# Decoder block on one core: adaLN shift and scale in groups of feature tiles, 32x32 VectorE transposes, another head order

## The chip, the cores and the metric

The kernel runs on one core of one Trainium2 chip. The time is device microseconds from the first to the last instruction of one launch, with what lies around it; the median of three runs before the change is 348.48 us (348.43 to 349.01). The core has five engines that run side by side, each with its own instruction stream: TensorE (PE, matrix products; the loading of its stationary operand is shown apart as PEld), VectorE (DVE), ScalarE (ACT), GpSimd (POOL) and SyncE (SP), which here only issues transfers from the device memory.

## The reference

One decoder block on 256 tokens of 1024 features, float32, one sequence:

```python
mod = silu(c) @ w_ada + b_ada                      # [6 * 1024], one vector for the sequence
sh1, sc1, gt1, sh2, sc2, gt2 = split(mod, 6)
h = rmsnorm(x, g_mix) * (1 + sc1) + sh1
q, k, v, u, c_gate, b_gate = split(h @ w_in)       # w_in [1024, 3072]
attn = causal attention(q, k, v), 8 heads of 64, with ALiBi slopes
conv = b_gate * causal_conv3(c_gate * u)
x = x + gt1 * (concat(rmsnorm(attn), rmsnorm(conv)) @ w_out)
h = rmsnorm(x, g_ffn) * (1 + sc2) + sh2
val, gte = split(causal_conv3(h @ w_up))           # w_up [1024, 5632]
x = x + gt2 * ((silu(gte) * val) @ w_down)         # w_down [2816, 1024]
return rmsnorm(x, g_final)
```

So every part waits for two things: a number for each token (the reciprocal root mean square) and a number for each feature (shift, scale, gate), which comes from a matrix-vector product with `w_ada` (24 MB in all).

## The kernel before

Everything is held as [feature, token]: the 1024 features are 8 K tiles of 128 partitions, the 256 tokens lie along the row. Large float32 products run as three passes in a faster format: each operand is split into `hi` (rounded; ScalarE makes it) and `lo` (the rest; VectorE makes it), and TensorE adds hi.hi, lo.hi and hi.lo (`mm3`, L200).

The block has three stages. **q, k, v**: K outermost, the 8 feature tiles of q and k and two token tiles of v accumulate in six PSUM banks while the K tiles arrive one after the other. **Mixer**: 12 steps of u, c, b tiles with one attention head beside each of the first eight, then 8 steps of w_out. **FFN**: 66 steps over pieces of w_up and w_down. All orders are written out by hand; each engine runs its instructions in the order of the program text. Weights go through one ring of eight [128, 2048] slots, filled by SP in the order of use; a slot's next transfer is issued once the engines have read its old content (`free`, `advance`).

What the change touches:

* **The head.** x is loaded in four transfers, then the packed parameters `par`. ScalarE squares x (`sqx`, L235), VectorE adds the squares, and TensorE sums them over the partitions (`pss`, L212: stationary the squares, 16 columns of ones moving). VectorE and POOL make the root `r` (L217, L219). To have it on every partition, VectorE multiplies the identity with it (`dg`, L223, two instructions), and TensorE multiplies ones with that (`psrx`, L228). `keep_clock` (L154) issues products whose result nobody reads.
* **adaLN for the mixer.** `ada_rows(kt, r)` (L263) makes one feature tile's shift and scale: silu(c), repeated over 32 columns (`crep`), is stationary, 256 columns of w_ada move. Four products run in the four groups of 32 columns of TensorE's array, each with its own two K tiles. The 512 KB halves of a feature tile's columns take one ring slot each. The result `psr` holds four partial sums in rows: ScalarE copies it to `ar` (L268), `ada_cols` transposes it with two TensorE products with the identity (`psc`, L274), VectorE adds the four (`red`, L276) and makes scale and shift per partition (`mod`, L277, L279).
* **Order in the q, k, v stage.** For each K tile TensorE runs 24 products of 256 columns (q, k) and 6 of 512 (v; one of its banks is named `warm`), and between them, for the next K tile, two calls of `ada_rows` and one `ada_cols`.
* **adaLN for the rest.** `mod_part` (L573) and `gate_part`/`gate_rows` (L553, L561) make sections of 1024 features in the same row form; `mod_copy` (L580) copies, `mod_cols` transposes with two TensorE products (L592) and adds the bias (L597, L601). Three of the four sections are turned in the mixer stage and at the FFN's start, one beside the FFN.
* **The two junctions.** Between mixer and FFN, and at the end, the chain runs pss, ms, r, dg, psrb (L228), then x times the root (`xnf` L285, `xT` L869). VectorE makes a piece of `lo` (L736) in between, or scales x by g_final.

In the tables one float32 product of the program is two MATMUL records and two LDWEIGHTS records; a product in the split format is one each. So the 8 products of an `ada_rows` pair are the 16 records of one L263 group.

Of the kernel before, what the change touches and what calls it, by code (L numbers as in the profile page):

```python
# [8 lines left out]
F32 = mybir.dt.float32  # L9
# [5 lines left out]
P = 128  # L15
S = 256
# [10 lines left out]
# columns of the packed per-feature parameters  # L27
# [8 lines left out]
# [128, 1024] pieces of the weights after q, k, v, in the order in which TensorE takes them  # L36
# [12 lines left out]
ADA_AHEAD = [(0, 0), (1, 1), (2, 2), (3, 3)] + [(k - 1, k) for k in range(4, KT)]  # L49
# [7 lines left out]
def decoder_block(ctx: ExitStack, tc, xT_in, pp, ada1, ada2, wqkv, wst, out):  # L57
    """One adaLN decoder block on 256 tokens, held as [feature, token] throughout.

    Large float32 products run as three float32r passes: an operand v is split exactly into  # L60
    hi = round(v) to float32r and lo = v - hi, which float32r holds too.
    """
# [22 lines left out]
    # ---------------------------------------------------------------- loads  # L85
    xT = cp.tile([P, KT, S], F32, name="xT")
    for i in range(4):
        nc.sync.dma_start(xT[:, 2 * i:2 * i + 2, :], xT_in[:, 2 * i:2 * i + 2, :])
    par = cp.tile([P, NP], F32, name="par")
    ffn_par = slice(PC["ffn_w"], NP)  # L90
    nc.sync.dma_start(par[:, 0:PC["ffn_w"]], pp[:, 0:PC["ffn_w"]])
# [5 lines left out]
    # one ring of [128, 2048] slots, filled in the order of use  # L97
    order = []
    for kt in range(KT):
        order += [("a1", k, i) for k in range(KT) for i in range(2) if ADA_AHEAD[k][i] == kt] + [("q", kt)]  # L100
# [8 lines left out]
    def advance():  # L109
        while state["next"] < len(order):  # L110
# [5 lines left out]
            if k[0] == "a1":  # L116
                nc.sync.dma_start(t[:, 0:1024], ada1[k[1], k[2]])
# [16 lines left out]
    # ------------------------------------------------------------ constants  # L134
# [14 lines left out]
    # TensorE's clock falls when it idles: products for nothing keep it up until the first weights are there  # L149
# [6 lines left out]
    keep_clock(15)  # L156

    # ------------------------------------------------- helpers
# [38 lines left out]
    def mm3(o, l, r, start, stop, shared=False, passes=(0, 1, 2)):  # L197
        """o (+)= (l_hi + l_lo).T @ (r_hi + r_lo) without lo.lo, which is below float32's rounding"""
# [16 lines left out]
    def rms_root(ss, n, name, beside=lambda: None):  # L215
# [4 lines left out]
        beside()  # L220
# [5 lines left out]
    def rms_bcast(dg, ps):  # L226
# [5 lines left out]
    pss = pw("pss")  # L232
    sqx = cp.tile([P, KT, S], F32, tag="mix", name="sqx")
    for i in range(4):
        ACT.activation(sqx[:, 2 * i:2 * i + 2, :], xT[:, 2 * i:2 * i + 2, :], AF.Square)  # L235
        if i:
            DVE.tensor_add(sqx[:, 0:2, :], sqx[:, 0:2, :], sqx[:, 2 * i:2 * i + 2, :])
    DVE.tensor_add(sqx[:, 0, :], sqx[:, 0, :], sqx[:, 1, :])
    add_squares(pss, sqx[:, 0, :], True, True)
    # silu(c), repeated over 32 columns as a stationary operand  # L240
# [8 lines left out]
    dgx = rms_root(pss, D, "x")  # L249
# [3 lines left out]
    mod1 = cp.tile([P, 2, KT], F32, name="mod1")      # scale, shift of the mixer's norm  # L253
# [3 lines left out]
    def ada_rows(kt, r):  # L257
        """half r of the K tiles: the column groups' K tiles are 2 j + r"""
        if r == 0:
            AR[kt] = pw(f"psr{kt}")  # L260
# [671 lines left out]
```

## Time and profile before

| | us |
|---|---|
| median of three runs | 348.48 (348.43 to 349.01) |
| span of the profiled execution | 347.5 |
| PE busy | 335.8 (97%) |
| PEld busy | 312.8 (90%) |
| DVE / ACT / POOL busy | 250.6 / 196.4 / 17.9 |

The profiled execution's own time lies 1.0 us above its span if it was a run of the median. Busy time of PE is not its peak, since products overlap; a stage is read from the starts of its products. The three stages begin at 16.08 us (first q product), 61.66 (first u product) and 147.84 (first product of the FFN); the last product of the FFN starts at 335.83.

### The profile page before, as it was taken

Reading aid. Unit: us, or ns where it says so; the run is one execution under the profiler, and the core shown is the slowest. Engines: PE = TensorE matmul, PEld = TensorE weight load, DVE = VectorE, ACT = ScalarE, POOL = GpSimd, SP = SyncE. Lnnn points to the kernel's source line nnn. Section 1 sums busy time; section 2 is a strip of 40 time slices with the busy share of each in tenths; the row PEclk is TensorE's granted clock in tenths of the full one; section 3 lists DMA queues with packets and bytes.
Section 4 is the critical chain, followed back from the end, with each engine's and each line's share of the span. In section 5 each row is a group of like instructions: output and inputs, shape, how many; then the busy total and the mean of one; then the engine's idle time right before and its main releaser. Section 6 shows DMA issues by size and latency. Waiting matters only on the chain.

```text
span 347.5 us, 6841 instructions
## 1 busy us (share of the span) xinstructions
PE 335.8 (97%) x2812; PEld 312.8 (90%) x2812; DVE 250.6 (72%) x443; ACT 196.4 (57%) x347; POOL 17.9 (5%) x31
## 2 busy tenths in 40 slices
PE   6999999999999999899999999999999999999992
PEld 6777778888788999699999999999999999999992
DVE  2647466497875887689878888888577777777754
ACT  5334355977776455558555555555555555555550
POOL 1000000001112100400000000000000000000020
PEclk9699999999999999999999999999999999999997
DMA  6999899878779567447536675757463642000003
GB/s 231 411 412 356 335 383 421 371 271 320 296 281 409 222 267 258 167 183 238 223 146 257 229 288 205 298 192 307 164 243 129 236 133 111 2 0 2 0 2 121
DMA packets 13854, 79.22 MB, mean 228 GB/s; under 512 B 1664, under 2 KB 2048, under 8 KB 6272
## 3 DMA queue, kind: packets, MB, share of 16 engines
q1 hardware_dynamic: 13824, 78.79, 60.0%
q8 instruction: 22, 0.36, 0.4%
q14 instruction: 8, 0.07, 0.1%
HBM read 77.74 MB, written 1.05 MB: 227 GB/s over the span
## 4 chain that ended last, share of the span: by engine, by line
PE 55%; DVE 1%; ACT 0%; DVEq 0%; issue 0%
PE pu L200 18%; PE pg L200 18%; PE pod L200 18%; PE pss L212 1%; DVE xT L869 1%; PE warm L154 0%; PE psrb L228 0%; DVE lo L736 0%; PE psg L561 0%; ACT hhi L287 0%; DVE xT L691 0%; DVE dg_x L223 0%; DVE xnf L285 0%; ACT sqr L693 0%; DVEq L928 0%
## 5 line engine op out<-in xcount | busy, mean ns | idle before, releaser
L166 DVE TENSOR_TENSOR lo<-raw,hi 128x1024 fp32r<-128x1024 f32 x85 | 103.9, 1228 | 3.0 <-ACT hi L161 3.0
L161 ACT CAST hi<-raw 128x1024 fp32r<-128x1024 f32 x86 | 88.7, 1040 | 0.0
L200 PE MATMUL pu<-hhi,hi 128*128 128x256 f32 x208 | 59.0, 284 | 1.0 <-ACT hhi L287 1.0
L200 PE MATMUL pu<-hhi,lo 128*128 128x256 f32 x208 | 58.2, 280 | 0.0
L200 PE MATMUL pu<-hlo,hi 128*128 128x256 f32 x208 | 57.9, 279 | 0.0
L200 PE MATMUL pod<-ahi,lo 128*128 128x256 f32 x176 | 49.5, 282 | 0.0
L200 PE MATMUL pod<-alo,hi 128*128 128x256 f32 x176 | 49.5, 281 | 0.0
L200 PE MATMUL pod<-ahi,hi 128*128 128x256 f32 x176 | 49.4, 281 | 0.0
L200 PE MATMUL pg<-hhi,hi 128*128 128x256 f32 x176 | 49.4, 280 | 0.0
L200 PE MATMUL pg<-hlo,hi 128*128 128x256 f32 x176 | 49.1, 279 | 0.0
L200 PE MATMUL pg<-hhi,lo 128*128 128x256 f32 x176 | 49.1, 279 | 0.0
L200 PEld LDWEIGHTS pu<-hhi,hi 128*128 128x128 f32 x208 | 39.0, 188 | 2.4 <-ACT hhi L287 1.2
L200 PEld LDWEIGHTS pu<-hhi,lo 128*128 128x128 f32 x208 | 39.1, 188 | 0.0
L200 PEld LDWEIGHTS pu<-hlo,hi 128*128 128x128 f32 x208 | 39.0, 188 | 0.0
L762 DVE SCALAR_TENSOR_TENSOR fyv<-pu,par,fyv 128x255 f32<-128x255 f32 (+1 forms) x44 | 21.2, 482 | 20.7 <-ACT fyv L756 19.9
L756 ACT ACTIVATE fyv<-pu,par 128x256 f32<-128x256 f32 x22 | 12.4, 564 | 40.6 <-PE pu L200 40.6
L200 PEld LDWEIGHTS pod<-ahi,lo 128*128 128x128 f32 x176 | 33.2, 188 | 0.0
L200 PEld LDWEIGHTS pod<-alo,hi 128*128 128x128 f32 x176 | 33.1, 188 | 0.0
L200 PEld LDWEIGHTS pod<-ahi,hi 128*128 128x128 f32 x176 | 33.1, 188 | 0.0
L200 PEld LDWEIGHTS pg<-hhi,lo 128*128 128x128 f32 x176 | 33.1, 188 | 0.0
L200 PEld LDWEIGHTS pg<-hhi,hi 128*128 128x128 f32 x176 | 33.0, 188 | 0.0
L200 PEld LDWEIGHTS pg<-hlo,hi 128*128 128x128 f32 x176 | 32.9, 187 | 0.0
(161 smaller groups left out, 664.4 us busy)
## 6 DMA issues: line engine op xcount, KB each, us to landing
raw<-in_wst SPq DMA_DIRECT2D x43, 1024.0 KB, 4.9
raw<-in_ada SPq DMA_DIRECT2D x16, 1024.0 KB, 6.6
raw<-in_ada SPq DMA_DIRECT2D x16, 512.0 KB, 6.1
raw<-in_wqkv SPq DMA_DIRECT2D x6, 768.0 KB, 7.4
xT<-in_x SPq DMA_DIRECT2D x4, 256.0 KB, 4.6
raw<-in_wqkv SPq DMA_DIRECT2D x2, 512.0 KB, 8.1
out<-xT SPq DMA_DIRECT2D x3, 256.0 KB, 2.7
raw<-in_wqkv SPq DMA_DIRECT2D x2, 256.0 KB, 8.2
```

What stands on the lines that cost most here:

```text
L161: ACT.copy(hi[:, 0:n], raw)
L166: DVE.tensor_sub(lo[:, 0:n], raw, hi[:, 0:n].bitcast(F32))
L200: PE.matmul(o, l[p == 2], r[p == 1], start=start and p == 0, stop=stop and p == 2, skip_group_check=shared)
L212: PE.matmul(ss[:, t * REP:(t + 1) * REP], s2[:, t * P:(t + 1) * P], ones[:, 0:REP], start=(first and t == 0), stop=last, skip_group_check= ...
L756: ACT.activation(Y[w, j], PU[w, j][:, 0:S], AF.Identity, bias=col("ffn_b", f), scale=col("ffn_w", 2 * 2 * NJ + f))
L762: DVE.scalar_tensor_tensor(y[:, d:], ps[:, 0:S - d], col("ffn_w", k * 2 * NJ + f), y[:, d:], op0=OP.mult, op1=OP.add)
L869: DVE.tensor_mul(xT[:, d, :], xT[:, d, :], rb3)
```

## The change

The columns of w_ada are laid out anew on the host, so that a row form of 32 partitions turns into a column form with one VectorE instruction that transposes 32x32 blocks; the TensorE transposes, the ScalarE copies and the reduction go. The mixer's shift and scale are made for groups of feature tiles, (0), (1), (2, 3), (4, 5), (6, 7): every column group of the array now runs over all 8 K tiles and holds 32 of each tile's 128 features, with 64 or 128 columns per product instead of 256. One ring slot holds 1 MB instead of 512 KB of this part. The root is broadcast by a stationary operand that repeats its one column 128 times, with the identity moving. In the head `par` is loaded first and from ScalarE's queue, silu(c) goes ahead of the squares, `ada_rows(0)` ahead of `pss`, and the numbers of clock-keeping products go from 15 and 7 to 22 and 4.

```diff
+GROUPS = [(0,), (1,), (2, 3), (4, 5), (6, 7)]
...
-    nc.sync.dma_start(par[:, 0:PC["ffn_w"]], pp[:, 0:PC["ffn_w"]])
+    nc.scalar.dma_start(par[:, 0:PC["ffn_w"]], pp[:, 0:PC["ffn_w"]])     # ahead of x
...
-        order += [("a1", k, i) for k in range(KT) for i in range(2) if ADA_AHEAD[k][i] == kt] + [("q", kt)]
+    for g, kts in enumerate(GROUPS):
+        order += [("a1", g, i) for i in range(len(kts))] + [("q", kt) for kt in kts]
...
-                nc.sync.dma_start(t[:, 0:1024], ada1[k[1], k[2]])
+                nc.sync.dma_start(t, ada1[GROUPS[k[1]][k[2]]])
...
-    keep_clock(15)
+    keep_clock(22)
...
-        dg = wk.tile([P, 2, P], F32, tag="dg", name=f"dg_{name}")
-        for t in range(2):
-            DVE.tensor_scalar(dg[:, t, :], ident, r[:, t:t + 1], None, op0=OP.mult)
-        return dg
+        return r
...
-            PE.matmul(ps[:, t * P:(t + 1) * P], ones, dg[:, t, :], start=True, stop=True)
+            PE.matmul(ps[:, t * P:(t + 1) * P], r[:, t:t + 1].to_broadcast([P, P]), ident, start=True, stop=True)
...
+    def ada_rows(g):
+        n = len(GROUPS[g])
+        AR[g] = pw(f"psr{g}")[:, 0:64 * n]
+        for k in range(KT):
+            a = ring["a1", g, k * n // KT].rearrange("p (k j c) -> p k j c", j=4, c=64 * n)
+            for j in range(4):
+                PE.matmul(AR[g][32 * j:32 * j + 32, :], crep[:, k, :], a[:, k % (KT // n), j, :],
+                          start=(k == 0), stop=(k == KT - 1))
+            if (k + 1) % (KT // n) == 0:
+                free(("a1", g, k * n // KT))
+    def ada_cols(g):
+        n, kts = len(GROUPS[g]), slice(GROUPS[g][0], GROUPS[g][-1] + 1)
+        tr = wk.tile([P, 256], F32, tag="tr", name=f"tr{g}")[:, 0:64 * n]
+        DVE.transpose(tr, AR[g])
+        v = tr.rearrange("p (n s q) -> p n s q", s=2, q=32)[:, :, :, 0]
+        b = PC["b_ada"] + kts.start
+        DVE.tensor_tensor(mod1[:, 0, kts], v[:, :, 1], bsc1[:, 0, kts], op=OP.add)
+        DVE.tensor_mul(mod1[:, 0, kts], mod1[:, 0, kts], par[:, PC["g_mix"] + kts.start:PC["g_mix"] + kts.stop])
+        DVE.tensor_tensor(mod1[:, 1, kts], v[:, :, 0], par[:, b:b + n], op=OP.add)
...
+    ada_rows(0)
+    add_squares(pss, sqx[:, 0, :], True, True)
+    rx = rms_root(pss, D, "x")
+    ada_cols(0)
+    keep_clock(4)
+    new_q(0)
+    for part in range(3):
+        split_hi_q(0, part)
+    split_lo_q(0, 0)
+    psrx = rms_bcast(rx, pw("psrx"))
     normed(0, psrx)
-    ada_cols(0)
-    keep_clock(7)
-    split_q(0, 0)
     modulated(0)
...
-            qk(kt, range(ROWS_AT[kt], COLS_AT[kt]))
-            if nxt:
-                ada_cols(kt + 1)
+            g = {1: 2, 3: 3, 5: 4}.get(kt)
...
+            if g:
+                ada_rows(g)
+                ada_cols(g)
+            qk(kt, range(4 if kt == 1 else 2, 8))
...
     def mod_cols(s):
-        for i in range(2):
-            PE.transpose(ps[:, i * P:(i + 1) * P], sacc[s, "ar"][:, i * P:(i + 1) * P], ident)
+        tr = wk.tile([P, 256], F32, tag="tr", name=f"trm{s}")
+        DVE.transpose(tr, sacc[s][:, 0:256])
+        v = tr.rearrange("p (k q) -> p k q", q=32)[:, :, 0]
...
-    dg2 = rms_root(pss2, D, "x2", lambda: lo_half(0))
+    r2 = rms_root(pss2, D, "x2")
+    lo_half(0)
+    mod_cols(1)
     lo_half(1)
...
-    h_scaled(0, rb2, mod2, "f", lambda: mod_cols(1))
+    h_scaled(0, rb2, mod2, "f")
```

On TensorE, the head up to the first q and k products stands before as follows (`warm` is the target of the clock-keeping products, `psr` the rows of shift and scale, `psc` their transposes, `pq` the banks of q and k):

```order
L154 MATMUL warm<-ones 128x128 x15
L212 MATMUL pss<-ones,sqx 128x16 x2
L263 MATMUL psr_168<-raw,crep 32x256 x8
L228 MATMUL psrx<-dg_x,ones 128x128 x2
L274 MATMUL psc_188<-ident,ar_181 128x128 x2
L154 MATMUL warm<-ones 128x128 x7
L200 MATMUL pq_163<-hhi,hi 128x256 x2
```

After the change the same place on TensorE reads:

```order
L155 MATMUL warm<-ones 128x128 x22
L261 MATMUL psr_165<-raw,crep 32x64 x32
L213 MATMUL pss<-ones,sqx 128x16 x2
L155 MATMUL warm<-ones 128x128 x4
L226 MATMUL psrx<-ident,r_x 128x128 x2
L201 MATMUL pq_161<-hhi,hi 128x256 x2
```

The rows of shift and scale moved ahead of the sum of squares and are 32 products of 64 columns instead of 8 of 256; the transposes are gone, and the broadcast is the last thing before q and k.

In the q, k, v stage, TensorE's work at the start of the third K tile reads before (`psr_367` are the rows of the fourth feature tile, `pq` again the banks of q and k):

```order
L200 MATMUL pq_163<-hhi,hi 128x256
L200 MATMUL pq_163<-hlo,hi 128x256
L200 MATMUL pq_163<-hhi,lo 128x256
L263 MATMUL psr_367<-raw,crep 32x256 x8
L200 MATMUL pq_164<-hhi,hi 128x256
L200 MATMUL pq_164<-hlo,hi 128x256
L200 MATMUL pq_164<-hhi,lo 128x256
```

After the change rows of two feature tiles stand in the second, fourth and sixth K tile only; in the second they read:

```order
L201 MATMUL pq_161<-hhi,lo 128x256 x2
L201 MATMUL pq_162<-hhi,lo 128x256 x2
L261 MATMUL psr_340<-raw,crep 32x128 x32
L201 MATMUL pq_163<-hhi,hi 128x256
L201 MATMUL pq_163<-hlo,hi 128x256
L201 MATMUL pq_163<-hhi,lo 128x256
```

Two groups of 8 products of 256 columns became one of 32 products of 128 columns, and no transposes follow on TensorE.

## Rows read from the trace of the kernel before

**Rows 1.** The page: its first line and the granted TensorE clock in 40 slices.
```profile
span 347.5 us, 6841 instructions
PEclk9699999999999999999999999999999999999997
```

**Rows 2.** Stretch, length, busy us (records) of PE, PEld, DVE, ACT, POOL; clock, DMA, GB/s.
```profile
16.05:61.80 45.75, 45.75 (x371) 35.88 (x370) 27.33 (x68) 21.30 (x42) 0.00 (x0) 1.00 0.97 383
5.70:9.10 3.40, 1.43 (x14) 1.24 (x12) 2.50 (x4) 3.10 (x5) 0.00 (x0) 1.00 0.98 363
9.10:12.50 3.40, 3.40 (x22) 2.09 (x23) 1.09 (x6) 0.65 (x3) 0.71 (x1) 0.50 1.04 419
...
145.60:149.05 3.45, 2.14 (x17) 1.90 (x17) 3.21 (x9) 1.47 (x4) 0.00 (x0) 1.00 0.86 313
```

**Rows 3.** Timeline of PE in the q, k, v stage: start us, length, what, records.
```profile
23.68 1.07 PE L263 MATMUL psr<-raw,crep 128*32 128x256 f32 x16
...
39.66 0.64 PE L263 MATMUL psr<-raw,crep 128*32 128x256 f32 x8
...
42.72 0.28 PE L200 MATMUL pq<-hhi,lo 128*128 128x256 f32 x1
42.84 0.38 PE L274 MATMUL psc<-ident,ar 128*128 128x128 f32 x2
42.97 0.36 PE L200 MATMUL pq<-hhi,hi 128*128 128x256 f32 x1
43.17 0.28 PE L200 MATMUL pq<-hlo,hi 128*128 128x256 f32 x1
...
45.62 0.64 PE L263 MATMUL psr<-raw,crep 128*32 128x256 f32 x8
...
57.43 0.28 PE L200 MATMUL pq<-hhi,hi 128*128 128x256 f32 x1
...
61.66 0.28 PE L200 MATMUL pu<-hhi,hi 128*128 128x256 f32 x1
```

**Rows 4.** Tile psr: weight loads, duration ns min/median/max, first and last start.
```profile
L263 PEld LDWEIGHTS psr<-raw,crep x128: 106/109/178, 10.0 to 53.1; 128*32 128x32 f32 x128
```

**Rows 5.** Timeline of the head, all engines; idle before and its releaser in brackets.
```profile
1.51 5.60 PE L154 MATMUL warm<-ones 128*128 128x128 f32 x30 [1.51 <-POOL mhalf L140]
10.05 1.94 PE L263 MATMUL psr<-raw,crep 128*32 128x256 f32 x16
10.47 0.71 POOL L219 TENSOR_TENSOR r_x<-ms_x,mhalf 128x2 f32<-128x2 f32 x1 [8.45 <-DVE ms_x L217]
13.18 0.42 DVE L295 TENSOR_TENSOR xna<-xT,psrx 128x256 f32<-128x256 f32 x1 [1.48 <-PE psrx L228]
13.36 2.97 PE L154 MATMUL warm<-ones 128*128 128x128 f32 x14
14.18 0.60 ACT L299 ACTIVATE hhi<-xna,mod 128x256 fp32r<-128x256 f32 x1 [1.24 <-DVE mod L279]
16.08 1.16 PE L200 MATMUL pq<-hhi,hi 128*128 128x256 f32 x8
```

**Rows 6.** Transfers issued at 3.5 us: tile 0's second w_ada half, us to landing.
```profile
raw<-in_ada SPq DMA_DIRECT2D x1, 512.0 KB, 6.5
```

**Rows 7.** Timeline of the junction at the end of the kernel.
```profile
338.68 1.58 PE L154 MATMUL warm<-ones 128*128 128x128 f32 x12
339.10 0.74 POOL L219 TENSOR_TENSOR r_x<-ms_x,mhalf 128x2 f32<-128x2 f32 x1 [2.15 <-DVE ms_x L217]
339.88 0.48 DVE L223 TENSOR_SCALAR dg_x<-ident,r_x 128x128 f32<-128x128 f32 x2
341.05 2.74 DVE L869 TENSOR_TENSOR xT<-xT,psrb 128x256 f32<-128x256 f32 x8 [0.68 <-PE psrb L228]
```

**Rows 8.** Timeline of the junction between mixer and FFN.
```profile
146.00 0.69 DVE L736 TENSOR_TENSOR lo<-raw,hi 128x512 fp32r<-128x512 f32 x1
147.28 0.91 ACT L287 ACTIVATE hhi<-xnf,mod 128x256 fp32r<-128x256 f32 x2 [1.24 <-DVE mod L601]
```

More of the change, by code (lines that the diff above doesn't have):

```diff
@@ L86, in decoder_block @@
     xT = cp.tile([P, KT, S], F32, name="xT")
+    par = cp.tile([P, NP], F32, name="par")
+    ffn_par = slice(PC["ffn_w"], NP)
+    nc.scalar.dma_start(par[:, 0:PC["ffn_w"]], pp[:, 0:PC["ffn_w"]])
     for i in range(4):
         nc.sync.dma_start(xT[:, 2 * i:2 * i + 2, :], xT_in[:, 2 * i:2 * i + 2, :])
-    par = cp.tile([P, NP], F32, name="par")
-    ffn_par = slice(PC["ffn_w"], NP)
-    nc.sync.dma_start(par[:, 0:PC["ffn_w"]], pp[:, 0:PC["ffn_w"]])
     def col(name, i):
@@ L219, in rms_root, with rms_bcast @@
         POOL.tensor_tensor(r, ms, mhalf, op=OP.pow)
-        beside()
-        dg = wk.tile([P, 2, P], F32, tag="dg", name=f"dg_{name}")
+        return r
+    def rms_bcast(r, ps):
         for t in range(2):
-            DVE.tensor_scalar(dg[:, t, :], ident, r[:, t:t + 1], None, op0=OP.mult)
-        return dg
-    def rms_bcast(dg, ps):
-        for t in range(2):
-            PE.matmul(ps[:, t * P:(t + 1) * P], ones, dg[:, t, :], start=True, stop=True)
-        return ps[:, 0:S]
[L232 to L239, printed above, removed]
+            PE.matmul(ps[:, t * P:(t + 1) * P], r[:, t:t + 1].to_broadcast([P, P]), ident, start=True, stop=True)
+        return ps[:, 0:S]
     cs = cp.tile([P, KT], F32, name="cs")
@@ L247, in decoder_block @@
     DVE.tensor_scalar(bsc1[:, 1, :], par[:, PC["b_ada"] + 32:PC["b_ada"] + 40], 1.0, None, op0=OP.add)
-    dgx = rms_root(pss, D, "x")
+    pss = p1("v", "pss")
+    sqx = cp.tile([P, KT, S], F32, tag="mix", name="sqx")
+    for i in range(4):
+        ACT.activation(sqx[:, 2 * i:2 * i + 2, :], xT[:, 2 * i:2 * i + 2, :], AF.Square)
+        if i:
+            DVE.tensor_add(sqx[:, 0:2, :], sqx[:, 0:2, :], sqx[:, 2 * i:2 * i + 2, :])
+    DVE.tensor_add(sqx[:, 0, :], sqx[:, 0, :], sqx[:, 1, :])
     rxb = cp.tile([P, S], F32, tag="sqs0", name="rxb")
@@ L255, in decoder_block @@
     AR = {}
-    def ada_rows(kt, r):
-        if r == 0:
-            AR[kt] = pw(f"psr{kt}")
-        a = ring["a1", kt, r].rearrange("p (k n) -> p k n", n=256)
-        for j in range(4):
-            PE.matmul(AR[kt][32 * j:32 * j + 32, 0:256], crep[:, 2 * j + r, :], a[:, j, :],
-                      start=(r == 0), stop=(r == 1))
-        free(("a1", kt, r))
-        if r == 1:
-            ar = wk.tile([P, 256], F32, tag="ar", name=f"ar{kt}")
-            ACT.copy(ar, AR[kt][:, 0:256])
-            AR[kt] = ar
-    def ada_cols(kt):
-        ps = pw(f"psc{kt}")
-        for i in range(2):
-            PE.transpose(ps[:, i * P:(i + 1) * P], AR[kt][:, i * P:(i + 1) * P], ident)
-        red = wk.tile([P, 2], F32, tag="red", name=f"red{kt}")
-        DVE.tensor_reduce(red, ps[:, 0:256].rearrange("p (i j r) -> p i j r", i=2, j=4)[:, :, :, 0], AX, OP.add)
-        DVE.scalar_tensor_tensor(mod1[:, 0, kt:kt + 1], red[:, 1:2], bsc1[:, 0, kt:kt + 1], col("g_mix", kt),
-                                 op0=OP.add, op1=OP.mult)
-        DVE.tensor_scalar(mod1[:, 1, kt:kt + 1], red[:, 0:1], col("b_ada", kt), None, op0=OP.add)
+    def ada_rows(g):
[17 more added lines that the diff above has]
+        DVE.tensor_tensor(mod1[:, 1, kts], v[:, :, 0], par[:, b:b + n], op=OP.add)
     XN = {}
@@ L305, in decoder_block, with new_q @@
     pq = [acc(f"pq{i}") for i in range(4)]
-    pv = [p1("v", "pv0"), warm]
+    pv = []
     WQ = {}
+    def new_q(kt):
+        WQ[kt] = [hip.tile([P, 1024], F32R, tag=t, name=t) for t in ("hi", "lo", "hi", "lo")]
     def split_q(kt, part):
-        raw = ring["q", kt]
         if part == 0:
-            WQ[kt] = [hip.tile([P, 1024], F32R, tag=t, name=t) for t in ("hi", "lo", "hi", "lo")]
-        hi, lo = WQ[kt][part // 2 * 2:part // 2 * 2 + 2]
-        c = slice((part % 2) * 512, (part % 2) * 512 + 512)
-        ACT.copy(hi[:, c], raw[:, part * 512:(part + 1) * 512])
-        DVE.tensor_sub(lo[:, c], raw[:, part * 512:(part + 1) * 512], hi[:, c].bitcast(F32))
-        if part == 2:
-            free(("q", kt))
+            new_q(kt)
+        split_hi_q(kt, part)
+        split_lo_q(kt, part)
     def qk(kt, tiles, passes=(0, 1, 2)):
@@ L889, in _arrange @@
     sec = w_ada.reshape(D, 6, D)
[L891 to L896 removed]
+    by_k = sec[:, 0:2].reshape(KT, P, 2, KT, 4, 32).transpose(1, 0, 4, 3, 2, 5)
+    ada1 = []
+    for kts in GROUPS:
+        n = len(kts)
+        a = by_k[:, :, :, kts[0]:kts[-1] + 1]
+        ada1 += [a[:, i * KT // n:(i + 1) * KT // n].reshape(P, 2048) for i in range(n)]
+    ada1 = np.stack(ada1)
+    ada2 = np.stack([sec[:, s].reshape(4, 2, P, KT, 4, 32).transpose(0, 2, 1, 4, 3, 5) for s in (2, 3, 4, 5)])
+    ada2 = ada2.reshape(4, 4, P, 2048)
     wqkv = w_in[:, :3 * A].reshape(KT, P, 3 * A)
```

96 lines of the change are left out of this document (38 added, 58 removed).

## The prediction

> **What bounds the kernel now.** I read the page first: its first line and the clock row say 347.5 us of span, nearly all of it at the full clock except the second slice and the end [rows 1]. Then the table by stretches: from 16 to 62 us, the q, k, v stage, PE is busy without a break and DMA at a share of 0.97, so both are near their limit [rows 2]. Last the timeline of PE there, read by starts, since products overlap: the last K tile, the only one without adaLN work beside it, runs from 57.43 to 61.66, 4.23 us; one with it lasts 5.96 us (39.66 to 45.62) [rows 3]. So the stage is bound by TensorE, and 1.73 us of such a K tile is adaLN. Whatever TensorE does less there moves the end, as the mixer and the FFN behind it are dense on TensorE too.
>
> **The price of adaLN in the loop, before.** Around the transposes three q starts in a row, 42.72, 42.97, 43.17, lie 0.45 us apart in all where two products alone need 0.24 (24 of them and 6 of twice the length make the 4.23): the two transposes cost 0.21. The rest of 1.73, 1.52 us, is two groups of rows, 0.76 each. A merged group of 16 records takes 1.07 us, one of 8 takes 0.64: 8 records more are 0.43, two rounds of four column groups at 0.215 each. So 0.43 of the 0.76 is columns and 0.33 goes into and out of the 32-column form. From 16.08 [rows 5] to 61.66 are 45.58 us; eight K tiles alone are 8 x 4.23 = 33.84; adaLN costs 11.74.
>
> **The price after.** Four groups stay in the loop: one of 64 columns and three of 128, each with 32 products, 64 records, 16 rounds. A round of 128 columns is half of 0.215: 16 x 0.1075 = 1.72. A round of 64 is 0.054, in all 0.86. That is the low end, where only columns count. The next end up: each round waits for its weight loads, which last 0.11 us [rows 4]: 16 x 0.11 = 1.76 for either size. I take 1.75 for 128 columns, where both ends meet, and for 64 the middle, 1.3, since no row is nearer to one end. The far end: each record costs what one costs now, 0.43 / 8 = 0.054 us, whatever its columns: 64 x 0.054 = 3.46. Loop after: 4 x 0.33 + 1.3 + 3 x 1.75 = 7.87, so 11.74 - 7.87 = 3.9 us less.
>
> The Trainium skill ("TensorE: Matmul & The Clock Gate", "Back-to-back issue gap") gives products of up to 64 columns a floor of about 25 ns from start to start. By it a round of four would need 0.1 us and the small group 1.6 us; by columns alone it is 0.86. Rows 3 show 0.054 us per record with 256 columns and can't decide between the two.
>
> **The head.** Before, `hhi`, the first thing the q products need, is ready at 14.78 (14.18 + 0.60), but the 14 records of clock-keeping stand from 13.36 to 16.33 in front of them, at half clock; q starts at 16.08 [rows 5]. After: 44 records instead of 30 keep PE until about 8.7 (1.51 + 5.60 + 14 x 0.12, the 0.12 from the 12 records in rows 7). The columns of tile 0 land, now as one transfer, when their second half does today, 3.5 + 6.5 = 10.0 [rows 6]; `par` ahead of x moves the same bytes. Rows from 10.1 for 1.3 plus 0.1 of change of form: 11.5. `pss`, four records of 0.12: 12.0. ms and hops 0.3, POOL's root 0.71: 13.0. Here `dg` is gone and four records of broadcast follow, 0.48 and 0.25 of tail: 13.75. xna 0.42, hhi 0.60, hops: 14.9. The four keep-clock products end before the root does. VectorE's transposition and three small operations fall beside POOL's root, and the `lo` piece behind them ends at about 13.7; a transposition is not in the trace, its nearest rows are xna (0.42, 256 columns from PSUM) and a tiny operation at 0.16, and from either end the start moves by less than 0.3. Gain 16.08 - 14.9 = 1.2 us, with bounds from 0.8 to 1.6 by the small group's two near ends.
>
> **Later transposes.** The three pairs that stand between dense products (two in the mixer, one beside the FFN) go: 3 x 0.21 = 0.65. VectorE's transposes there take up to 0.42 each beside TensorE; ScalarE loses its copies.
>
> **The end.** `dg` lies on the chain, 0.48, between the root's end (339.84) and the broadcast [rows 7]. After, the broadcast stands behind the clock products, whose 12 records last to about 340.1; with 0.48 and the tail, x is scaled from 340.87 instead of 341.05: 0.2 us, between 0 and 0.48.
>
> **Mixer to FFN.** `dg` leaves VectorE's chain, but the transposition with its addition (0.42 + 0.16) now stands ahead of the second `lo` piece (0.69) and of xnf; hhi came at 147.28 and will come there again, give or take 0.3 [rows 8]. I put 0.
>
> **Sum.** 1.2 + 3.9 + 0.65 + 0.2 = 5.95 off a span of 347.5: 341.55. The median, 348.48, is 0.98 above the span, so 342.5 us. For its own range I take the ends for the small group and the head, 341.3 to 343.8.
>
> **Rivals.**
> *Rounds wait for loads.* Each round lasts 0.11 us [rows 4]. The two small groups, one in the head and one in the loop, cost 1.76 instead of 1.3: 343.4. For it speaks that a load lasts longer than 64 columns need; against it that loads and products overlap in the present groups. By the Trainium skill's floor (same page and section) such a group would take 1.6, nearly this case.
>
> *The clock falls in the head.* Before, from 5.70 to 9.10, PE was busy for 1.43 of 3.40 us, with 2 us of nothing at its end, and was granted 0.50 (1.2 GHz) from 9.10 on, though it was then busy throughout [rows 2]; it was back at 2.4 GHz at 16.05, after the keep-clock products. After, PE has nothing to do from 8.7 to 10.1 and from 13.5 to 14.9. Against it: from 145.60 to 149.05 it was busy 2.14 of 3.45 and kept 1.00. If the clock falls, the broadcast takes 0.5 longer, and the first q products run at half speed for 3 to 4 us, somewhat longer than the keep-clock products needed (2.97 [rows 5]), of which half is lost: 2 us in all, 344.5.
>
> *DMA is late.* The rows of tiles 2 and 3 need both their slots, 6.87 MB in the queue's order (x 1.05, `par` 0.05, four slots of w_ada at 1.05, two of q, k, v weights at 0.79): the first 2.15 MB by 10.0, the other 4.72 MB at 419 GB/s [rows 2] by 21.3. TensorE asks at 14.9 + 4.23 + 0.33 + 1.3 + 1.41 (half a q, k part) = 22.2. A margin of 0.9 us; if transfers ran at the stage's mean of 383 GB/s it would be 0.1 short. All later groups have more. Price: up to 2 us, 344.5.
>
> *Slower: each record costs 0.054 us, however few its columns.* Then five groups of 64 records take 3.46 each. The head starts q 2.16 later than I said, at 17.1, and the loop's adaLN is 4 x (0.33 + 3.46) = 15.2, 3.4 more than now. With 0.85 off behind, 347.5 + 1.0 + 3.4 - 0.85 = 351.05, 352.0 us. It decides from 2.75 us per group, 0.043 per record, on. For it: no row shows PE issuing records faster than this for long, and the records of this part rise from 128 to 320. Against: the 0.215 of a present round is what 256 columns, passed twice, need at 2.4 GHz (512 / 2.4 = 213 ns), so the rate is that of columns.
>
> **How the numbers follow.** Forecast 0.50, loads 0.12, clock 0.20, DMA 0.05, slower 0.13. A measurement tells 0.2%, 0.7 us, from no change. Faster: all but the slower case and a part of the DMA case where other waits add up, 0.85; same 0.02; slower 0.13. The range leaves out the slower case and some 0.07 at both ends: 341.2 to 346.0.
>
> **What would show it.** In the profile after: psr groups of 64 records of 1.3 us (64 columns) and 1.75 us (128), by the starts of the products around them, with K tiles 3, 5, 7 and 8 at 4.23; the first q product at 14.9 and the first u product at 56.5; the clock at 1.00 from 9 to 16 us; the last FFN product 5.75 earlier. I am wrong if a group of 128 columns takes over 2.7 us, if q starts after 16, or if PE waits for a landing before the tiles 2 and 3.

## The result and the profile after

The changed kernel takes 343.42 us (median of 342.16, 343.33, 343.52, 343.58) beside 348.75 for the kernel before (348.43 to 349.46): a ratio of 0.9834 [0.981, 0.9858]. Forecast were 342.5 us, between 341.2 and 346.0. The profiled execution is the one of 342.16 us. The page of the kernel after answers to [rows 1]: the span and the rows of 40 slices for PE and its granted clock.

```profile
span 340.3 us, 7158 instructions
...
PE   8799999999999999899999999999999999999992
...
PEclk9999999999999999999999999999999999999998
```

The second slice, at a mean of 0.6 before, is now at the full clock, as is all the rest up to the last broadcast. By the starts of products, the stages compare so (us):

| | before | after | less | forecast |
|---|---|---|---|---|
| first q product | 16.08 | 14.82 | 1.26 | 1.2 |
| q, k, v, to the first u product | 45.57 | 41.23 | 4.34 | 3.9 |
| mixer, to the first FFN product | 86.19 | 85.54 | 0.65 | 0.42 |
| FFN, to its last product | 187.98 | 187.32 | 0.66 | 0.21 |
| tail | 11.67 | 11.43 | 0.24 | 0.2 |
| span | 347.5 | 340.35 | 7.15 | 5.95 |

First the head, in the timeline of all engines (start and duration in us, engine, line, operation, tiles, count). It answers to [rows 5].

```profile
10.20 1.10 PE L261 MATMUL psr<-raw,crep 128*32 128x64 f32 x64 [1.06 <-DMA raw<-in_ada]
11.23 0.62 PE L213 MATMUL pss<-ones,sqx 128*128 128x16 f32 x4
11.96 0.24 DVE L270 STREAM_TRANSPOSE tr<-psr 128x64 f32<-128x64 f32 x1
12.20 0.70 POOL L220 TENSOR_TENSOR r_x<-ms_x,mhalf 128x2 f32<-128x2 f32 x1 [10.18 <-DVE tr L270]
12.96 0.71 PE L226 MATMUL psrx<-ident,r_x 128*128 128x128 f32 x4
13.71 0.42 DVE L291 TENSOR_TENSOR xna<-xT,psrx 128x256 f32<-128x256 f32 x1 [0.44 <-PE psrx L226]
14.16 0.60 ACT L295 ACTIVATE hhi<-xna,mod 128x256 fp32r<-128x256 f32 x1 [1.14 <-DVE xna L291]
14.82 0.39 PE L201 MATMUL pq<-hhi,hi 128*128 128x256 f32 x1 [1.15 <-ACT hhi L295]
```

The reader is to see the chain landing, rows, `pss`, root, broadcast, `xna`, `hhi`, and that the last bracket of the q product names `hhi`: no clock-keeping product stands before it any more, so POOL's 0.70 and the two hops around `xna` set the time.

Then the loop, in PE's timeline of the same kernel: one group of 64 columns, one of 128, and the first u product. It answers to [rows 3].

```profile
15.96 1.10 PE L261 MATMUL psr<-raw,crep 128*32 128x64 f32 x64
16.99 1.18 PE L201 MATMUL pq<-hlo,hi 128*128 128x256 f32 x8
...
20.30 0.63 PE L201 MATMUL pq<-hhi,hi 128*128 128x256 f32 x4
...
21.80 1.95 PE L261 MATMUL psr<-raw,crep 128*32 128x128 f32 x64
23.69 0.39 PE L201 MATMUL pq<-hhi,hi 128*128 128x256 f32 x1
...
56.05 0.28 PE L201 MATMUL pu<-hhi,hi 128*128 128x256 f32 x1
```

From the first row of a group to the next q product are 1.03 us with 64 columns and 1.89 with 128. The first K tile, which carries the small group, lasts from 14.82 to 20.30, 5.48 us, 1.25 above the 4.23 of one without adaLN.

Between mixer and FFN the timeline after answers to [rows 8]:

```profile
138.20 1.14 POOL L220 TENSOR_TENSOR r_x<-ms_x,mhalf 128x2 f32<-128x2 f32 x1 [1.98 <-DVE ms_x L218]
139.35 0.45 DVE L585 STREAM_TRANSPOSE trm<-psm 128x256 f32<-128x256 f32 x1 [0.56 <-PE psm L574]
139.40 0.71 PE L226 MATMUL psrb<-ident,r_x 128*128 128x128 f32 x4
139.92 0.68 DVE L724 TENSOR_TENSOR lo<-raw,hi 128x512 fp32r<-128x512 f32 x1
140.52 0.87 DVE L281 SCALAR_TENSOR_TENSOR xnf<-xT,mod,psrb 128x256 f32<-128x256 f32 x2
```

The broadcast starts with the root's end and runs beside VectorE's transposition; `xnf` starts as VectorE finishes `lo` (139.92 + 0.68), 0.4 us after TensorE has made `psrb`. At the end, the answer to [rows 7]:

```profile
332.26 0.74 POOL L220 TENSOR_TENSOR r_x<-ms_x,mhalf 128x2 f32<-128x2 f32 x1 [2.20 <-DVE ms_x L218]
333.19 0.61 PE L226 MATMUL psrb<-ident,r_x 128*128 128x128 f32 x4
333.90 0.75 DVE L859 TENSOR_TENSOR xT<-xT,psrb 128x256 f32<-128x256 f32 x2 [0.93 <-PE psrb L226]
```

From the root's end (333.00) to the broadcast is 0.19 us, in place of `dg` and its hop.

So the profiled execution answers to the forecast, but the other three have spans of 341.5 to 341.8, 1.2 to 1.5 us longer, and only means of 0.97 to 0.99 of the granted clock. Where these runs lose, and what the changes of each part are worth by themselves, the experiments have to say. Medians below are over all runs of a kernel, while the ratios leave out runs over 1.5% longer than the kernel's fastest.

### The profile page after: what moved, and what is told of

It reads as the page before. It is cut to its first block, busy times and chain, and to the rows that moved or that the text cites. A ratio compares the mean times of both kernels' runs of the same rounds, so it can differ in the third digit from the quotient of the medians.

```text
span 340.3 us, 7158 instructions
## 1 busy us (share of the span) xinstructions
PE 328.0 (96%) x2988; PEld 312.6 (92%) x2988; DVE 249.7 (73%) x433; ACT 190.9 (56%) x334; POOL 18.9 (6%) x31
## 4 chain that ended last, share of the span: by engine, by line
PE 93%; DMA 2%; DVE 2%; SPq 0%; ACT 0%; issue 0%; POOL 0%; DVEq 0%
PE pu L201 22%; PE pg L201 18%; PE pod L201 18%; PE pq L201 7%; PE pox L201 7%; PE pc L201 4%; PE pb L201 3%; PE psm L574 2%; PE psr L261 2%; DMA raw<-in_ada 2%; PE warm L201 2%; PE pv L201 2%; PE pss L213 1%; PE pss L455 1%; PE pss L454 1%; PE pso L502 1%
## 5 line engine op out<-in xcount | busy, mean ns | idle before, releaser
L752 DVE SCALAR_TENSOR_TENSOR fyv<-pu,par,fyv 128x255 f32<-128x255 f32 (+1 forms) x44 | 21.2, 482 | 22.1 <-ACT fyv L746 21.3
```

The lines of the kernel that those rows point to most:

```text
L752: DVE.scalar_tensor_tensor(y[:, d:], ps[:, 0:S - d], col("ffn_w", k * 2 * NJ + f), y[:, d:], op0=OP.mult, op1=OP.add)
```

## The experiments

**The clock in the head (a_clock).** The changed kernel with more clock-keeping products in the head.

```diff
-    keep_clock(22)
+    keep_clock(26)
...
     psrx = rms_bcast(rx, pw("psrx"))
+    keep_clock(5)
```

> The changed kernel with more clock-keeping products in its two idle stretches of the head: 26 instead of 22 at the start, 5 more between the root's broadcast and the first q product. If the 1.2 us between the profiled execution of the changed kernel (342.2 us) and its other three (343.3 to 343.6) are TensorE's clock falling in the head in most executions, all executions come to 342.0 to 342.4 and the mean granted clock to 0.996. Rival: the difference comes from elsewhere (transfers); then the median stays at 343.4 and the executions go on differing.

Measured: 345.63, 343.57, 346.38, 339.03, 345.59, 343.31 us (median 344.58, ratio 0.9787 [0.9738, 0.9836]). The expectation failed: the runs scatter more than those of the changed kernel. The profiled one starts q at 14.55 and ends the loop at 55.94, both fine; it loses at the two junctions. The table by stretches (busy time of each engine, then the granted clock, DMA share and GB/s), first of this kernel, then of the changed one around the FFN's start:

```profile
139.50:141.65 2.15, 0.67 (x5) 0.48 (x5) 1.93 (x6) 0.73 (x2) 0.00 (x0) 1.00 0.80 316
141.65:145.07 3.42, 3.42 (x17) 3.42 (x18) 3.28 (x8) 1.70 (x4) 0.00 (x0) 0.50 0.96 405
329.50:332.80 3.30, 2.98 (x27) 2.78 (x25) 1.66 (x4) 2.70 (x8) 1.47 (x2) 1.00 0.00 0
332.80:336.00 3.20, 3.20 (x16) 3.20 (x16) 0.94 (x4) 1.24 (x4) 0.74 (x1) 0.50 0.00 0
```
```profile
139.50:141.65 2.15, 0.67 (x5) 0.48 (x5) 1.93 (x6) 0.62 (x2) 0.00 (x0) 1.00 0.76 278
141.65:145.07 3.42, 3.42 (x29) 3.42 (x30) 3.28 (x8) 1.82 (x4) 0.00 (x0) 1.00 1.00 414
```

The code of the junction is the same and PE was busy for the same 0.67 of 2.15 us before it; one run is then granted 0.50 (1.2 GHz) and has 17 products in 3.42 us, the other 1.00 and 29. The FFN takes 188.85 instead of 187.32, the tail 13.51 instead of 11.43: 1.5 and 2.1 us for the two falls.

**One part undone in before, and one part added to it (b_noclock, b_cols).** The kernel before without the seven clock-keeping products ahead of q; and the kernel before with VectorE's transposes for the three later sections.

```diff
-    keep_clock(7)
```
```diff
-    mod_copy(1)
+    mod_cols(1)
...
+        DVE.transpose(tr, sacc[s][:, 0:256])
```

> The kernel before without the 7 clock-keeping products that stand between the mixer's first transposes and the first q products. Both theories: the first q product starts at 14.8 instead of 16.08 us. If the 1.3 us that these products hold up q was all there was to gain in the head, 1.3 us faster than before (347.4). Rival, the clock: without them q runs at half the clock for some 3 to 4 us, and the time is 0.3 to 1.0 us above before (349.0 to 349.7).

> The kernel before, with the three sections behind the q, k, v stage and the FFN's shift turned by 32x32 transposes on VectorE (the layout of these columns changed with it), nothing else of the change. Theory: three pairs of TensorE transposes go from between dense products, 3 x 0.21 = 0.65 us: 347.8 to 348.0. Rival one: the VectorE transposes delay what stands behind them and take it back: no change. Rival two: the whole gain seen behind the q, k, v stage (1.6 us) comes from this part: 347.1.

Measured: 350.20 (348.5 to 350.91), ratio 1.0011 [0.9995, 1.0026], for the first; 349.81 (348.26 to 352.62), 1.0024 [0.9997, 1.0052], for the second. Neither is faster than the kernel before, whose runs beside them have a median of 349.36, so both expectations of a gain (347.4 and 347.8 to 348.0) failed. In the profile of b_noclock q does start right behind `hhi`, but at 16.04: the last squares came 1.6 us later in this execution, and TensorE was at 0.50 from 11.14 to 14.55, so this profile can't show what the products alone cost. b_cols needs 55.68 us from the first u product to the first w_out product, 0.45 less than before with its two transposes (0.42 forecast), and 6.80 from the last w_out product to the first of the FFN, 0.39 more than before, since there `dg` (0.48) and the transposition (0.44) stand in one row on VectorE, ahead of `lo` and `xnf`:

```profile
144.66 0.48 DVE L223 TENSOR_SCALAR dg_x<-ident,r_x 128x128 f32<-128x128 f32 x2 [0.59 <-POOL r_x L219]
145.06 0.44 DVE L584 STREAM_TRANSPOSE trm<-psm 128x256 f32<-128x256 f32 x1
146.22 0.86 DVE L285 SCALAR_TENSOR_TENSOR xnf<-xT,mod,psrb 128x256 f32<-128x256 f32 x2
```

Then its clock falls from 147.74 to 151.15, at the FFN's start.

**What sets the length of a group (a_single).** The changed kernel with eight groups of one feature tile each.

```diff
-GROUPS = [(0,), (1,), (2, 3), (4, 5), (6, 7)]
+GROUPS = [(i,) for i in range(KT)]
```

> The changed kernel with groups of one feature tile throughout: 7 groups of 64 columns in the loop instead of one of 64 and three of 128; same columns, 3 more changes of form, 192 more records. Theory (columns set the rounds, 0.33 us per group for going into and out of the 32-column form): 3 x 0.33 = 1.0 us slower than the changed kernel. Rival, only columns count: no difference. Rival, each record costs time of its own (0.02 us beyond its columns): 3.8 us more, 4.8 us slower in all.

Measured: 343.77 (342.78 to 348.38), ratio 0.9829 [0.9804, 0.9854]; the loop takes 42.17 us, 0.94 more than 41.23. In PE's timeline the groups that carry a single tile last as long as the first:

```profile
21.66 1.10 PE L261 MATMUL psr<-raw,crep 128*32 128x64 f32 x64
22.69 0.39 PE L201 MATMUL pq<-hhi,hi 128*128 128x256 f32 x1
```

Three groups and 192 records more cost 0.94 us, 0.31 a group: that is the change of form alone (0.33 in the prediction). If each record had cost 0.054 us, it would have been 10 us. So columns set the length, and the change of form comes on top.

**The broadcast through dg again (a_dg).**

```diff
-            PE.matmul(ps[:, t * P:(t + 1) * P], r[:, t:t + 1].to_broadcast([P, P]), ident, start=True, stop=True)
+            DVE.tensor_scalar(dg[:, t, :], ident, r[:, t:t + 1], None, op0=OP.mult)
...
+            PE.matmul(ps[:, t * P:(t + 1) * P], ones, dg[:, t, :], start=True, stop=True)
```

> The changed kernel with the root broadcast as before (VectorE scales the identity, dg, 2 x 0.24 us, and ones are stationary). If dg lies on the chain as I reckoned: in the head the broadcast starts 0.5 us later, so the first q product at 15.3 instead of 14.82; at mixer to FFN dg (0.5) is ahead of the broadcast, but the chain there ends in VectorE's second lo piece and xnf, so the first FFN product is 0.3 to 0.5 later against the first u product; at the end 0.2 to 0.3 later. In all 1.0 to 1.3 us longer where the clock is the same. The rival, that dg hides beside POOL and TensorE: the stages last as in the changed kernel, to 0.1.

Measured: 340.1, 343.1, 344.54, 348.33 us, ratio 0.9802 [0.9758, 0.9846]. The profiled run, of 340.1 us, is faster than any of the first four of the changed kernel, though each of the three places is later: q at 15.21 (0.39 later, less than the 0.5 expected), the mixer stage 85.87 (0.33 longer), the tail 11.65 (0.22 longer). The head in its timeline:

```profile
12.28 0.70 POOL L220 TENSOR_TENSOR r_x<-ms_x,mhalf 128x2 f32<-128x2 f32 x1 [10.26 <-DVE tr L276]
13.02 0.48 DVE L226 TENSOR_SCALAR dg_x<-ident,r_x 128x128 f32<-128x128 f32 x2 [0.27 <-POOL r_x L220]
13.36 0.71 PE L232 MATMUL psrx<-dg_x,ones 128*128 128x128 f32 x4 [0.45 <-DVE dg_x L226]
...
15.21 0.39 PE L201 MATMUL pq<-hhi,hi 128*128 128x256 f32 x1 [1.15 <-ACT hhi L301]
```

The root ends 0.08 us later here than in the changed kernel's first profile, so 0.31 of the 0.39 are `dg`. A start of q moves with the landing of the first columns anyway: the unaltered kernel starts it at 14.50 in a_same (below), where they landed at 9.74 instead of 10.06. So leaving `dg` out is worth 0.86 us over the three places; the expected 1.0 to 1.3 were too much. The run is short for another reason: its FFN takes 184.23 us instead of 187.32. Up to `psg3`, the four products of the last gate at 238 us, it keeps step with the changed kernel; behind it a step of 24 products takes 2.72 us instead of 2.83, to the end, at a granted clock of 1.00 in both. Products of 256 columns follow each other at 113.3 ns here and at 117.8 there.

**Is that rhythm the kernel's, or drawn in each run (a_same, a_break)?** The changed kernel once more, unaltered; and the kernel a_keep (below) with four more products in the form of `psg3` early in the FFN.

```diff
+        if n == 6:
+            ps6 = pw("break6")
+            for j in range(4):
+                PE.matmul(ps6[32 * j:32 * j + 32, 0:256], ones[:, 0:32], zt[:, 0, 0:S], start=True, stop=True)
```

> The changed kernel once more, for the spread of its runs. In the profiles so far the products of 256 columns of the FFN follow each other at 117.8 ns up to psg3 (the four products of the last gate), and behind it at 117.8 in some kernels and at 113.3 in others, with the granted clock at 1.00 in both: 187.3 or 184.2 us for the stage. If that rhythm is drawn anew in every run, some of these runs lie 3 us below the others, at 339 to 340. If it belongs to the kernel (the changed one has the slow rhythm, those with other heads the fast one), all lie between 342 and 344.

> The kernel with the products at the junctions, and in the FFN behind the first piece of w_down four more products in the form of psg3 (32 columns stationary, 256 moving), whose result nobody reads. If an interruption of this form lets the rhythm change: products at 113.3 ns from there (158 us) to psg3, 3.1 us less, minus 0.5 for the four products, 338.5 to 339.5 in those runs that keep it behind psg3 too. If the rhythm is set by the place or the time in the run: 117.8 up to psg3 as before, and 0.5 us more than without, 342.2.

Measured: a_same 339.28, 340.13, 340.51, 345.94, 347.5, 347.75 (ratio 0.9732 [0.969, 0.9773]); a_break 342.19 to 343.32 (median 342.65). The tables by stretches, of PE and PEld up to POOL as above, ahead of `psg3` and behind it; first the changed kernel's first profile, then a_same, then a_break:

```profile
165.00:236.00 71.00, 71.00 (x605) 71.00 (x604) 59.87 (x84) 40.00 (x60) 0.00 (x0) 1.00 0.66 242
241.00:320.00 79.00, 79.00 (x673) 79.00 (x673) 56.72 (x84) 44.46 (x65) 0.00 (x0) 1.00 0.28 99
```
```profile
165.00:236.00 71.00, 71.00 (x605) 71.00 (x604) 59.65 (x83) 40.04 (x60) 0.00 (x0) 1.00 0.66 240
241.00:320.00 79.00, 79.00 (x700) 79.00 (x699) 58.92 (x87) 46.49 (x68) 0.00 (x0) 1.00 0.28 101
```
```profile
165.00:236.00 71.00, 71.00 (x629) 71.00 (x628) 60.54 (x86) 40.82 (x60) 0.00 (x0) 1.00 0.66 243
241.00:320.00 79.00, 79.00 (x673) 79.00 (x673) 57.05 (x84) 44.48 (x65) 0.00 (x0) 1.00 0.27 99
```

PE counts as busy throughout and the clock is 1.00 in all six; only the number of products differs: 605 or 629 in 71 us, 673 or 700 in 79. The same program has either rhythm, so behind `psg3` it belongs to the run; in these profiles it changes where a group in column form interrupts the dense products (at 164 us in a_break, at 238 in a_same) and then holds to the next interruption. The slow one costs 3.1 us between `psg3` and the end. In a_break's profile the fast one came at the new group and was lost again at `psg3`; its FFN takes 185.50. None of its six runs comes to the 338.5 to 339.5 expected of one that keeps it, so that the new group is the cause rests on one profile, and what decides the draw isn't settled. The rest of a_same's scatter fits the clock: its profile shows 0.50 from 329.44 to 332.86, and a tail of 12.67, and its three long runs, which have no profile, have mean clocks of 0.975 to 0.985.

**The sum of squares ahead of the rows (a_pss).**

```diff
-    ada_rows(0)
     add_squares(pss, sqx[:, 0, :], True, True)
     rx = rms_root(pss, D, "x")
+    ada_rows(0)
...
-    split_lo_q(0, 0)
     psrx = rms_bcast(rx, pw("psrx"))
     normed(0, psrx)
+    split_lo_q(0, 0)
```

So the edit also puts `xna` ahead of the first `lo` piece; no run parts the two moves.

> The changed kernel with the sum of squares and the root ahead of the rows of tile 0, which land only at 10.06: pss fits in TensorE's wait, and the root (0.7 on POOL) beside the rows. If the head is the chain rows, pss, root, broadcast: first q product at 13.7 to 14.0 instead of 14.82. What the later stage makes of it by the landings: the second half of the columns for tiles 2 and 3 lands at 22.0 and is then asked for at 21.0, so about 1.0 of the gain is given back as a wait in the loop, and the first u product comes within 0.3 of 56.05. By the rival, a loop bound by TensorE alone, the first u product comes at 55.0.

Measured: 341.99 to 345.95, ratio 0.9857 [0.9814, 0.99]. q starts at 13.72, 1.10 earlier (its rows start 0.26 earlier, at 9.94); the first u product comes at 55.74, 0.31 earlier. Where most of the rest goes stands in PE's timeline at the group for tiles 2 and 3:

```profile
20.79 1.08 PE L261 MATMUL psr<-raw,crep 128*32 128x128 f32 x32
22.26 1.08 PE L261 MATMUL psr<-raw,crep 128*32 128x128 f32 x32 [0.39 <-DMA raw<-in_ada]
```

The second half of the group starts 1.47 us after the first, where the changed kernel's first profile has 0.90, since its columns land only at 22.22: the transfers that were nobody's wait there become one as soon as q starts early. The unaltered kernel meets it too: in a_same, with q at 14.50, they land at 22.64 and the second half starts 1.12 after the first.

**The clock at the junctions (a_keep).** The five products of a_clock in the head, and clock-keeping products of 512 columns at both junctions.

```diff
     rb2 = rms_bcast(r2, acc("psrb2"))
+    keep_wide(3, pw("warm2"))
...
-    finish(1, pd, last_down, pss3, lambda b: None, lambda: None, (4, 5, 0, 6, 7))
+    finish(1, pd, last_down, pss3, lambda b: None, lambda: keep_wide(1, warm3), (4, 5, 0, 6, 7))
-    keep_clock(6, pw("warm3"))
+    keep_wide(3, warm3)
```

> The changed kernel with five more clock-keeping products behind the broadcast in the head, three of 512 columns behind the broadcast between mixer and FFN, and in the tail one of 512 ahead of pss and three of 512 instead of the six of 128. If the falls of the granted clock at the two junctions are what parts the runs: the granted clock stays at 1.00 from 16 us to the last broadcast, FFN 187.3 and tail 11.4 us, and the runs agree within 1 us around 342.0. If the spread comes from elsewhere: the runs still lie 2 us or more apart though the profile shows a clock of 1.00 at both junctions. If the products don't hold the clock: 0.50 for some 3.4 us behind one of them, as in the other kernels, at 1.5 to 2 us.

Measured: 341.07, 341.24, 341.71, 341.77, 341.83 and 344.28 us (median 341.74), ratio 0.9785 [0.9759, 0.9811]. The mean granted clock of all six is 0.996 to 0.998, that of an execution without a fall, and the profiled one shows none before the last broadcast; five agree within 0.8 us. The profiled one has the fast rhythm (FFN 184.53); the sixth, 2.5 us longer at a clock of 0.998, has the length of the slow one, though without a profile that is inferred. So the clock and the rhythm are enough to account for the scatter. That the median comes near the 342.0 expected is luck: the fast rhythm gives back what the products cost. That price was mis-sized: a product of 512 columns is two records that follow each other at 0.43 us, and the tail's row shows what they delay.

```profile
329.49 2.82 PE L161 MATMUL warm<-zt,ones 128*128 128x512 f32 x6
332.15 0.61 PE L230 MATMUL psrb<-ident,r_x 128*128 128x128 f32 x4
```

The root was ready at 330.73; the broadcast waits for the six records until 332.15. The tail lasts 12.91 us, the mixer stage 86.07 (0.5 more).

**All together (a_best, a_fin).** `pss` ahead of the rows, `xna` ahead of the first `lo` piece, the groups (0), (1), (2), (3), (4, 5), (6, 7), and the wide products of a_keep at the junctions, with one clock-keeping product instead of four ahead of the broadcast in the head. a_fin has two more at the start and four behind the broadcast, two wide ones between mixer and FFN, and in the tail two small ones ahead of `pss`, one wide and two small behind it. With it the changed kernel ran on the same chip (a_same2). Part of a_fin's edit:

```diff
-GROUPS = [(0,), (1,), (2, 3), (4, 5), (6, 7)]
+GROUPS = [(0,), (1,), (2,), (3,), (4, 5), (6, 7)]
...
+    psrx = rms_bcast(rx, pw("psrx"))
+    keep_clock(4)
+    normed(0, psrx)
     split_lo_q(0, 0)
-    psrx = rms_bcast(rx, pw("psrx"))
-    normed(0, psrx)
...
-    keep_clock(6, pw("warm3"))
+    keep_wide(1, warm3)
+    keep_clock(2, warm3)
```

> All together: the sum of squares ahead of the rows of tile 0, xna ahead of the first lo piece, groups (0), (1), (2), (3), (4, 5), (6, 7) so that no group waits for two transfers early, and the clock-keeping products at both junctions. First q product at 13.6 (1.2 earlier than the changed kernel); one more group, 0.33 more in the loop, 41.6; the stages behind as in the changed kernel. In all 0.9 us faster than it: span 339.5, about 341.3. By the rival (transfers bind the early loop) the first u product comes no earlier than 56.0 and the time is that of the changed kernel.

> The version with all together, and the clock-keeping products at the junctions cut to what the waits hold. A product of 512 columns took 0.86 us (two records of 0.43), twice what I had reckoned, so three of them put the last broadcast 1.4 us and the first FFN product 0.4 later. Now two between mixer and FFN; in the tail two of 128 columns ahead of pss, and one of 512 and two of 128 behind it (1.3 us, as the six of 128 before). If the clock holds: first q product at 13.4, first u product at 55.2, mixer stage 85.7, tail 11.5, span 337 with the fast rhythm behind psg3 and 340 with the slow one; the median near 339.5. If so few products don't hold the clock: 0.50 for some 3.4 us behind a junction in the profile or in half of the runs, 1.5 to 2 us more each, and runs up to 344.

> The changed kernel on the same chip, as the measure for the run above. As before: 339 to 341 where the clock holds and the rhythm behind psg3 is fast, 342 to 343 with the slow one, and 1.5 to 2 us more for each fall of the clock. The version above lies 2 to 3 us below its median if its gains add up (head 1.2, one group more -0.33, falls 1 to 2 on average).

Measured: a_best 340.52 to 344.5 (median 341.57), ratio 0.9788 [0.9753, 0.9822], q at 13.38, first u product at 55.19; its profile has the fast rhythm (FFN 184.53) and the tail of a_keep (12.94), so its nearness to the 341.3 expected is luck too, and two of its six runs have mean clocks of 0.985 and 0.993. a_fin 340.91, 341.19, 341.33, 342.25 (median 341.26), 0.9775 [0.9756, 0.9795]; a_same2 341.37 to 347.92 (median 344.57), 0.9858 [0.9839, 0.9878]. In a_fin the mean clock is 0.995 to 0.997 in all runs, and the stages are those of the changed kernel (mixer 85.54, tail 11.41) with q at 13.45 and a loop of 41.79. Its profile has the slow rhythm, and no run is short enough for the fast one, so the median stayed 1.8 above the 339.5 that I expected; it is 3.3 below that of a_same2, of which 0.8 are the head less the longer loop (1.37 - 0.56; one more group was reckoned at 0.33) and the rest fits falls of the clock that it avoids: the unprofiled runs of a_same2 have mean clocks of 0.975 to 0.990. This is the version that I would keep, though by a margin that the rhythm, which neither controls, can hide in a few runs.

The profile of a_same2 shows another place where the clock can fall. PE's timeline in the head, then the table by stretches:

```profile
13.37 1.06 PE L226 MATMUL psrx<-ident,r_x 128*128 128x128 f32 x4
15.58 2.07 PE L201 MATMUL pq<-hhi,hi 128*128 128x256 f32 x8 [1.15 <-ACT hhi L295]
```
```profile
8.00:12.07 4.07, 2.24 (x75) 1.99 (x74) 1.22 (x4) 0.91 (x3) 0.00 (x0) 1.00 1.03 425
12.07:18.90 6.83, 5.68 (x72) 5.16 (x74) 4.02 (x12) 1.90 (x5) 0.70 (x1) 0.50 1.02 415
```

PE was busy for 2.24 of the 4.07 us before, and was granted 0.50 from 12.07 to 18.90. q starts 0.76 later than in the first profile and the loop takes 1.58 more: 2.34 us at the first u product. The run is the shortest of the six all the same (341.37), as its FFN has the fast rhythm (184.23).

## Why the prediction was right

The forecast held, by its own mechanism, and in part by luck. One term was mis-sized (the small group), one effect stood in no term (the rhythm of the dense products), and the time around the span was taken too short, which hid the other two. The steps gave 1.20 us more than the sum, the time around the span took 0.83 back, and the unprofiled runs lie 1.2 to 1.4 us above the profiled one: so the median came out 0.9 above the forecast.

**The loop (3.9 forecast, 4.34 measured).** The term that was off is the small group: 1.3 us for its 16 rounds, the middle between columns alone (0.86) and weight loads (1.76). Sixteen rounds last 0.90: the records come in fours that start 56 ns apart, the low end. The three groups of 128 columns cost 2.05 each against 0.33 + 1.75 = 2.08. So loads overlap even where a load (0.11 us) is twice as long as the columns that it serves; a_single confirms it with 128 such rounds. This settles the rival "rounds wait for loads", and "slower: each record costs 0.054 us", which a_single would have shown with 10 us. No run has the new groups with the old transposes in the loop, so the transposes' share of the 4.34 rests on the 0.21 a pair read from [rows 3]. The Trainium skill's floor of about 25 ns from start to start ("TensorE: Matmul & The Clock Gate", "Back-to-back issue gap") doesn't hold across column groups here: the four records of a round start 7 ns apart, and the measurement decides.

**The head (1.2, measured 1.26).** The steps are those of the prediction: `xna` at 13.71 (13.75 forecast), q at 14.82 (14.9). The rows were 0.37 shorter than reckoned, the landing and the hops to the root and to `xna` 0.33 longer in all, so the sum is better than its parts. a_dg shows `dg` at 0.31 (0.48 forecast), and a_pss that the order had more to give: with `pss` in the wait for the landing and `xna` ahead of `lo`, q comes at 13.72.

**Mixer (0.42 forecast, 0.65 measured).** (With 0.21 in the FFN, this is the prediction's 3 x 0.21, which is 0.63 and not 0.65.) To the first w_out product 0.71 us go: b_cols gives 0.45 of them to the two transposes, with the same rhythm as before. The other 0.26 is that rhythm: four stretches of 11 products and one of 26 run at 113 ns in the changed kernel and at 117 to 118 before, and one of 11 the other way round (59 products by 4.4 ns are 0.26). From the last w_out product to the first of the FFN are 6.48 us instead of 6.41: the prediction's "0" held, and for its reason: `dg` (0.48) leaves VectorE's row, the transposition and its addition (0.44 and 0.17 in b_cols) join it. Undone alone, `dg` costs 0.32 there (6.80 in a_dg), added alone the transposition 0.39 (6.80 in b_cols), and both together nearly nothing.

**FFN (0.21 forecast, 0.66 measured).** The dense products average 118.03 to 118.09 ns from start to start in the profile of before and 117.78 in that of after, over some 1,560 of them 0.43 us; the remaining 0.22 appears at once behind `psg3`, where the pair of transposes stood. All three profiles of the kernel before and its variants have the longer spacing, and none of the changed kernel and its variants; why, the runs don't show.

**The tail** gave 0.24 (0.2), a_dg's 0.22 of it by `dg`.

**The time around the span.** I took 0.98 us, by the median of before; each execution that shows both has 1.7 to 1.9, 1.81 here. That hides most of what the steps gave more: 347.5 - 7.15 + 1.81 = 342.16, where 342.5 was said.

**The rivals.** "The clock falls in the head" was priced at 2 us, 344.5, with a chance of 0.20: a_same2 shows it at a cost of 2.34. It is not in the changed kernel's first profile. I had not seen that the same can happen at both junctions: two of the changed kernel's three profiles show one fall, one in the head, one in the tail. In the tail of [rows 7], too, the clock does not hold in every execution: b_noclock, with before's own tail, falls there from 338.82 to 342.23. That the median is 343.4 and not 342.2 fits falls in the three unprofiled runs: mean clocks of 0.987 are some 9 us at half clock in two of them, and 0.972 is 19 us in the third, where the first profile has 2.6. That the third is the shortest all the same would fit the fast rhythm beside its falls. These runs have no profile, so number and places are open. "DMA late": the margin that I reckoned as 0.9 us was 0.7 in the first profile (the columns landed at 22.00, not 21.3, and were asked for at 22.70) and none in a_same, where q started 0.32 earlier and the landing came 0.64 later; a_pss has 0.39 us of idle time that the row names.

The range held, since it covered clock falls by one of the rivals; for the rhythm, which moves runs by 3.1 us, it had no term. A fast draw gave 339.3 to 340.5 in a_same, below its lower end.

## What to carry to other kernels

Price small products in column groups by columns, a round of four as one (shown here for 64 and 128 columns), and add the change of form for each group (0.31 to 0.33 us here): that decides how many groups a split may have. Where one edit takes a link out of an engine's chain and another puts one in, price the place as a whole: between mixer and FFN each alone is worth 0.3 to 0.4 us, and together nothing. When a kernel's runs differ by more than the effect, compare the stages of profiles and the granted clock of each stretch before the medians: three measurements of this one kernel gave ratios of 0.9834, 0.9732 and 0.9858, the second with an interval clear of the other two, though its median of 343.22 is close to the first one's 343.42 (344.57 in the third). Their runs mix two rhythms with falls of the clock.

## What the runs showed of the hardware

- Two rhythms of dense products of 256 columns, 113.3 and 117.8 ns from start to start, at a granted clock of 1.00 in both; in the FFN a run keeps one until a group in column form interrupts the stream.
- Products in four column groups start in rounds of four records, 7 ns apart, a round every 56 ns for 64 float32 columns, with weight loads of 0.11 us fully beside them.
- A VectorE transposition of 32x32 blocks from PSUM takes 0.24 us for 64 columns, 0.32 for 128 and 0.44 for 256.
- The granted clock can go to 0.50 behind the same instructions, equally busy, that leave it at 1.00 in another execution (0.67 of 2.15 us busy in both); with the waits filled by products its mean was 0.995 or more in all ten runs of a_keep and a_fin, and in five of the six of a_break (0.992 in the other), which has the same products as a_keep.
